# Reordering the first loads and spreading the norms, transposes and mixing of a decoder step on eight cores

## The chip, the cores and the metric

The program runs on all 8 NeuronCores of one Trainium2 chip, two dies of four cores. Every core runs the same instructions on its own batch element; the cores do not talk to each other. The time of one execution is the device time of the slowest core. Executions of one kernel mostly agree within 0.3%. There is a second, slower state, in which the cores of one die are granted a lower TensorE clock; runs in that state are set apart and only fast runs are compared with fast runs.

Engines in the profile: PE is TensorE (matmul), PEld its weight loads, DVE VectorE, ACT ScalarE, POOL GpSimd, SP the engine that issues most DMAs. L344 and so on are lines of the kernel; most operations go through helpers, so L344 is simply "a matmul", L347 "a transpose on TensorE", L362 a scalar_tensor_tensor on VectorE, L366 a copy by ScalarE.

## The reference, cut to what matters

One layer of a decoder. Per core: 2048 prompt rows and 128 sample rows of width 1024.

```python
h = rmsnorm(x, g_mix)
z = h @ w_in                       # u | v | p | q | gate_logits
u = gelu(u); vhat = layernorm(gelu(v), g_v, b_v)
a = (u * (tril(w_s[g]) @ vhat + b_s[g])) @ w_out_a       # per 128-row chunk, 4 groups
b = multiscale_pool(p, ...) @ w_out_b                    # trailing means, 2..16 rows
c = attend(q, memory K/V) @ w_out_c
x = x + (sig(g_a)*a + sig(g_b)*b + sig(g_c)*c) @ w_o
x = x + relu(rmsnorm(x) @ w_up)**2 @ w_down
y = rmsnorm(x, g_final)
```

The part that matters here is the first stage: rmsnorm of rows, then the projections v, q, p, u, and the spatial mixing. The bulk of the time (merge, `w_o`, MLP) is the same code in both kernels, but for the order in which the attention of the sample rows is slotted into the merge.

## The kernel before: the parts that the argument touches

Rows come in tiles of 128 (`x` tile t, 512 KB), four tiles to a block. For each tile: ScalarE squares and sums, VectorE and GpSimd make the reciprocal root (`norm_a`, `norm_b`), VectorE scales (`N`), TensorE transposes and an engine evicts the transpose, that is, copies it out of the matmul bank, into `hT` (`T`). Weights come in 30 chunks (2 MB in memory, cast to 1 MB by the DMA) into four slots; the first three are v, pq (p and q) and u. Chunks are issued from GpSimd's queue; rows and constants from SP's queue.

```python
def load_next(expect=None, after=()):
    # ... slot of the next chunk ...
    s.dma("pool", [(slots[sl][:, :], wpk[CH[nm]])], writes=[slot_b[sl]], owner=slot_b[sl], after=after)

def norm_load(t, src, after=()):
    xt, xb = ring("xst", xst, xst_b)                 # four row buffers
    s.dma("sp", [(xt, src)], writes=[xb], owner=xb, after=after)

def trans(t, dst, dst_bufs, col0, eng):              # T(t): eight transposes, one eviction
    for k in range(8):
        TR(b16[:, k*128:(k+1)*128], xn[:, k*128:(k+1)*128], [xnb], [bk_b])
    CP(eng, dst[:, :, col0:col0+128], ..., [bk_b], dst_bufs)

# start: constants, row 0, the norm gain broadcast to 128 partitions (512 KB), rows 1 to 3
s.dma("sp", [(bnd[:, B_ID:B_ID+128], cb[...])], ...)      # identity for the transposes
s.dma("sp", [(cstt[:], cst)], ...)                        # small constants
norm_load(0, xrow(0))
s.dma("sp", [(gb[:], gvec[0].partition_broadcast(128))], ...)
for t in BT[0][1:]:
    norm_load(t, xrow(t))
load_next("v", after=[cst_b])
# ...
for i in range(4):
    nb = norm_a([i]); norm_b(*nb)                    # statistics of row i
    if i >= 1:
        N(i - 1); T(i - 1)                           # scale and transpose row i-1
N(3)
load_next("pq", after=[slot_b[0]])                   # waits until v has landed
load_x(BT[1]); setup_loads(); mem_loads()
vmm(0); T(3)
for i in range(1, 4): vmm(i)                         # projection V
vfin()
load_next("u", after=[slot_b[1]])                    # waits until pq has landed
# ... Q(0), P(0..3), WIN(0), then the four U groups, with T(4..7) in between
```

`wpk`, `x` and so on are tensors in HBM. `after` makes the issuing queue wait for a landing. In these traces VectorE takes its instructions in program order, and that will matter: after the change row 0 has landed at 4.7 us, but VectorE scales it only at 31.5 us, just behind the statistics of row 1 (31.3 us), which stand before it in the program.

The softmax here doesn't subtract the row's maximum and nothing guards it: scores larger than these inputs give would overflow.

## Time and profile before

Median 977.1 us (975.6 to 977.5). The profiled execution, slowest core (core 7):

```profile
PE 915.6 (94%) x5312; PEld 472.1 (48%) x5312; DVE 383.7 (39%) x644; ACT 306.2 (31%) x535; POOL 267.7 (27%) x274
...
PE   0768889999999999999999999999999999999996
...
DMA  8891533804094122234050130402104040130134
```

The first line is the page's busy time of each engine in us, its share of the span and its instructions. The two others are 40 equal slices of the span (24 us each), one digit a slice, in tenths busy. TensorE is at 9 tenths or more nearly everywhere; it is open only in the first six slices, and at the very end, which the change does not touch. In the first two slices the DMA engines are nearly full.

The longest waits of TensorE up to 60.3 us (total us, number of waits, longest), and the chain of waits that ended last, from 0 to 62 us (start, us, what; longest pieces):

```profile
PE bank L347 <- DVE X L362: 25.3, 3, 18.3
PE bank L344 <- DMA slot<-wpk: 11.2, 2, 7.2
```

```profile
3.38 17.79 DMA X<-x
...
27.53 14.35 DMA slot<-wpk
...
42.42 17.68 DMA slot<-wpk
60.23 1.87 PE bank L344 x4
```

`X<-x` is the load of a row, `slot<-wpk` the load of a weight chunk, `bank` a bank of TensorE's output. Read the chain from the top: the third row (17.8 us to land), then chunk pq, then chunk u, one after the other, and only then the U groups can run. The timeline of TensorE shows the same two waits, and what a restart costs (columns: start, us, operation, count; in brackets the idle time before it and what ended it):

```profile
42.02 5.30 PE L344 MATMUL bank<-hT,slot 128*128 128x512 bf16 x16 [4.01 <-DMA slot<-wpk]
...
60.23 3.57 PE L344 MATMUL bank<-hT,slot 128*128 128x512 bf16 x8 [7.20 <-DMA slot<-wpk]
...
64.08 1.89 PE L344 MATMUL bank<-hT,slot 128*128 128x512 bf16 x8
```

The same eight matmuls take 3.6 us right after a 7.2 us wait and 1.9 us later. The Trainium skill ("TensorE: Matmul & The Clock Gate", Part 1) says that an idle TensorE falls back to half its clock and needs a few microseconds of work to get it back; this trace agrees, with a factor of 1.9 and a granted clock of 0.50 from 56.8 to 63.7 us.

### The profile page before, as it was taken

Reading aid. Unit: us, or ns where it says so; the run is one execution under the profiler, and the core shown is the slowest. Engines: PE = TensorE matmul, PEld = TensorE weight load, DVE = VectorE, ACT = ScalarE, POOL = GpSimd, SP = SyncE. Lnnn points to the kernel's source line nnn. Section 1 sums busy time; section 2 is a strip of 40 time slices with the busy share of each in tenths; the row PEclk is TensorE's granted clock in tenths of the full one; section 3 lists DMA queues with packets and bytes.
Section 4 is the critical chain, followed back from the end, with each engine's and each line's share of the span. In section 5 each row is a group of like instructions: output and inputs, shape, how many; then the busy total and the mean of one; then the engine's idle time right before and its main releaser. Section 6 shows DMA issues by size and latency. Waiting matters only on the chain.

```text
span 973.8 us, 15566 instructions; the slowest of 8 cores (967.0 to 973.8 us)
## 1 busy us (share of the span) xinstructions
PE 915.6 (94%) x5312; PEld 472.1 (48%) x5312; DVE 383.7 (39%) x644; ACT 306.2 (31%) x535; POOL 267.7 (27%) x274
## 2 busy tenths in 40 slices
PE   0768889999999999999999999999999999999996
PEld 0344555444555555545555544554445544455442
DVE  1366675423333322235532244222442234322476
ACT  2214454675322222225553200232003310033332
POOL 1103222614343343443332300222002310032243
PEclk9989999999999999999999999999999999999998
DMA  8891533804094122234050130402104040130134
GB/s 184 192 224 44 131 66 72 173 1 87 2 240 74 33 44 44 45 92 147 1 110 1 17 71 1 87 1 47 40 1 87 1 85 3 23 65 1 44 152 173
DMA packets 16536, 70.73 MB, mean 73 GB/s; under 512 B 1981, under 2 KB 3004, under 8 KB 12620
## 3 DMA queue, kind: packets, MB, share of 16 engines
q0 software_dynamic: 5472, 35.65, 20.6%
q1 hardware_dynamic: 10988, 34.09, 10.7%
q8 instruction: 44, 0.72, 0.3%
q14 instruction: 32, 0.26, 0.1%
HBM read 95.28 MB, written 10.22 MB: 108 GB/s over the span
## 4 chain that ended last, share of the span: by engine, by line
PE 88%; DMA 5%; DVE 2%; ACT 1%; issue 1%; POOL 1%; DVEq 0%; SPq 0%; POOLq 0%; ACTq 0%
PE bank L344 87%; DMA slot<-wpk 3%; DMA X<-x 2%; PE bank L347 1%; ACT X L350 1%; DVE X L362 1%; POOL stats L353 1%; ACT L350 0%; DVE X L359 0%; DVE CR L362 0%; DVE X L368 0%; DVE stats L547 0%; SPq L156 0%; DVEq L128 0%; DVE X L353 0%
## 5 line engine op out<-in xcount | busy, mean ns | idle before, releaser
L344 PE MATMUL bank<-hT,slot 128*128 128x436 bf16 (+3 forms) x2480 | 471.1, 349 | 12.9 <-DMA slot<-wpk 11.2
L344 PEld LDWEIGHTS bank<-hT,slot 128*128 128x128 bf16 x2480 | 240.3, 98 | 228.0 <-issue 20.9
L344 PE MATMUL bank<-slot,CR 128*128 128x512 bf16 (+1 forms) x1376 | 298.5, 378 | 0.1
L350 ACT ACTIVATE fA<-bank 128x436 f32<-128x436 f32 (+2 forms) x215 | 116.2, 544 | 361.6 <-PE bank L344 324.1
L344 PEld LDWEIGHTS bank<-slot,CR 128*128 128x128 bf16 x1376 | 134.0, 98 | 157.2 <-issue 0.2
L362 DVE SCALAR_TENSOR_TENSOR X<-bank,stats,X 128x512 f32<-128x512 f32 x136 | 102.0, 750 | 119.8 <-PE bank L344 119.8
L350 ACT ACTIVATE fW<-bank 128x436 f32<-128x436 f32 (+2 forms) x103 | 54.7, 533 | 166.4 <-PE bank L344 164.7
L353 POOL TENSOR_TENSOR CR<-fA 128x436 bf16<-128x436 f32 (+1 forms) x69 | 66.5, 964 | 109.1 <-ACT fA L350 104.8
L353 DVE TENSOR_TENSOR CR<-fA 128x436 bf16<-128x436 f32 (+1 forms) x51 | 31.2, 612 | 115.7 <-ACT fA L350 115.7
L353 DVE TENSOR_TENSOR fA<-bank,fA 128x436 f32<-128x436 f32 (+1 forms) x77 | 42.7, 603 | 79.8 <-PE bank L344 79.7
L353 POOL TENSOR_TENSOR stats<-stats,cstt 128x1 f32<-128x1 f32 (+3 forms) x30 | 35.4, 1181 | 119.4 <-DVE stats L359 77.9
L156 POOL DMA_DIRECT2D slot<-wpk x30 | 17.2, 573 | 182.8 <-PE bank L344 174.4
L350 ACT ACTIVATE CC<-X 128x1024 bf16<-128x1024 f32 x34 | 35.9, 1057 | 76.1 <-DVE stats L359 36.8
L344 PE MATMUL bank<-X,slot 128*128 128x436 bf16 (+1 forms) x240 | 57.1, 347 | 2.4 <-DVE X L353 2.0
L353 POOL TENSOR_TENSOR CR<-fW 128x436 bf16<-128x436 f32 (+1 forms) x37 | 35.1, 948 | 63.1 <-ACT fW L350 61.3
L344 PE MATMUL bank<-slot,hT 128*128 128x512 bf16 (+1 forms) x272 | 48.4, 334 | 2.1 <-DVE fA L362 1.2
L353 DVE TENSOR_TENSOR X<-bank,X 128x512 f32<-128x512 f32 (+2 forms) x39 | 26.7, 685 | 49.9 <-PE bank L344 25.5
L353 POOL TENSOR_TENSOR fA<-fA 128x436 f32<-128x436 f32 (+1 forms) x22 | 24.3, 1103 | 79.8 <-DVE fA L353 79.8
L353 DVE TENSOR_TENSOR CR<-fW 128x436 bf16<-128x436 f32 (+1 forms) x29 | 17.7, 612 | 66.7 <-ACT fW L350 66.7
L347 PE MATMUL bank<-bnd,X 128*128 128x128 bf16 x152 | 14.0, 242 | 29.6 <-DVE X L362 28.6
L353 DVE TENSOR_TENSOR fW<-bank,fW 128x436 f32<-128x436 f32 (+1 forms) x43 | 24.1, 603 | 42.8 <-PE bank L344 42.8
L344 PEld LDWEIGHTS bank<-slot,hT 128*128 128x128 bf16 x272 | 26.6, 100 | 21.6 <-issue 5.9
(90 smaller groups left out, 492.0 us busy)
## 6 DMA issues: line engine op xcount, KB each, us to landing
slot<-wpk POOLq DMA_DIRECT2D x30, 1024.0 KB, 12.2
X<-x SPq DMA_DIRECT2D x34, 512.0 KB, 8.5
y<-hT SPq DMA_DIRECT2D x17, 512.0 KB, 2.7
CR<-ck POOLq DMA_DIRECT2D x4, 512.0 KB, 8.4
CR<-cv POOLq DMA_DIRECT2D x4, 512.0 KB, 10.8
gb<-gvec SPq DMA_DIRECT2D x3, 512.0 KB, 9.1
CR<-mem SPq DMA_DIRECT2D x2, 512.0 KB, 24.2
fW<-wst SPq DMA_DIRECT2D x2, 256.0 KB, 12.3
```

The lines of the kernel that those rows point to most:

```text
L156: eng.dma_start(out=o_ap, in_=i_ap).then_inc(owner.sem, 16)
L344: s.op("pe", lambda e: e.matmul(out, lhsT=lhsT, rhs=rhs, start=start, stop=stop), R_, W_)
L347: s.op("pe", lambda e: e.transpose(out=out, in_=in_, identity=identb), R_ + [ident_b], W_)
L350: s.op("act", lambda e: e.activation(out=out, in_=in_, func=func, **kw), R_, W_)
L353: s.op(eng, lambda e: e.tensor_tensor(out=out, in0=in0, in1=in1, op=op), R_, W_)
L362: s.op("dve", lambda e: e.scalar_tensor_tensor(out=out, in0=in0, scalar=scalar, in1=in1, op0=op0, op1=op1), R_, W_)
```

## The change

Intent: keep TensorE fed in the first 270 us. (1) The first three weight chunks are queued at once, at the very start, on GpSimd's queue; row 0 goes out before them, rows 1 to 3 behind them on SP's queue. (2) The 512 KB broadcast of the norm gain becomes a 4 KB row, which TensorE spreads over the partitions with two f32 matmuls against a row of ones; the 512 KB of broadcast bias rows is treated alike, with one-row f32 matmuls that add the bias into the spatial-gate constants. (3) Norms, transposes (many now evicted by ScalarE) and mixing are spread between the projections. (4) Set-up loads move behind what is needed first. The core of the diff:

```diff
+        onef = CC[1][0:1, 0, :]                      # a row of ones
+        norm_load(0, xrow(0))
+        grow = oT[0:1, 0, 0:2048].bitcast(F32)
+        s.dma("sp", [(grow, gvec[0].unsqueeze(0))], writes=grow_b, owner=grow_b[0])
+        load_next("v")
+        load_next("pq")
+        load_next("u")
+        s.dma("sp", [(cstt[:], cst)], writes=[cst_b], owner=cst_b)
         s.dma("sp", [(bnd[:, B_ID:B_ID + 128], ...)], ...)
-        s.dma("sp", [(cstt[:], cst)], writes=[cst_b], owner=cst_b)
-        norm_load(0, xrow(0))
-        s.dma("sp", [(gb[:], gvec[0].partition_broadcast(128))], ...)
         for t in BT[0][1:]:
             norm_load(t, xrow(t))
-        load_next("v", after=[cst_b])
+        for n in range(2):                           # gain row -> 128 partitions
+            MM(bk[:, :], onef, grow[:, n*512:(n+1)*512], True, True, ...)
+            CP("act", gb[:, n*512:(n+1)*512], bk[:, :], [bk_b], [gb_b])
 ...
+        def setup_mm(i):
+            for g in range(4):
+                MM(o, bvb[:, g*128:(g+1)*128], wsf[i][:, g, :], True, False, ...)
+                MM(o, onef, bsrow[:, i*512 + g*128:...], False, True, ...)
 ...
-        load_next("pq", after=[slot_b[0]])
-        load_x(BT[1])
+        load_x(BT[1][0:2], after=[slot_b[1]])
         setup_loads()
-        mem_loads()
+        load_x(BT[1][2:4], after=[slot_b[2]])
 ...
-        load_next("u", after=[slot_b[1]])
 ...                                                  # the block loop, written out:
+        us.append(U(1, 2))
+        T(nx[0], "act")
+        MIX(1, 1, *us[1])
+        ...
```

The loop over the first four rows (`norm_a`, `norm_b`, `N(i-1)`, `T(i-1)`) is unchanged.

More of the change, by code (lines that the diff above doesn't have):

```diff
@@ L457, in build_program @@
         BT = [[0, 1, 2, 3], [4, 5, 6, 7], [8, 9, 10, 11], [12, 13, 14, 15]]
+        onef = CC[1][0:1, 0, :]
+        MEMSET("dve", onef, 1.0, [CC_b[1]])
+        norm_load(0, xrow(0))
+        grow = oT[0:1, 0, 0:2048].bitcast(F32)
+        grow_b = oT_b[0][0:4]
+        s.dma("sp", [(grow, gvec[0].unsqueeze(0))], writes=grow_b, owner=grow_b[0])
[3 more added lines that the diff above has]
+        s.dma("sp", [(cstt[:], cst)], writes=[cst_b], owner=cst_b)
         s.dma("sp", [(bnd[:, B_ID:B_ID + 128], cb[:, B_ID:B_ID + 128])], writes=[ident_b], owner=ident_b)
-        s.dma("sp", [(cstt[:], cst)], writes=[cst_b], owner=cst_b)
-        norm_load(0, xrow(0))
-        s.dma("sp", [(gb[:], gvec[0].partition_broadcast(128))], writes=[gb_b], owner=gb_b)
         for t in BT[0][1:]:
             norm_load(t, xrow(t))
-        x_b = [norm_src[t][1] for t in BT[0]]
-        load_next("v", after=[cst_b])
         MEMSET("pool", ones, 1.0, [ones_b])
         MEMSET("pool", qbd, 0.0, [qbd_b])
+        for n in range(2):
+            bk, bk_b = pb()
+            MM(bk[:, :], onef, grow[:, n * 512:(n + 1) * 512], True, True, grow_b + [CC_b[1]], [bk_b])
+            CP("act", gb[:, n * 512:(n + 1) * 512], bk[:, :], [bk_b], [gb_b])
         wst_t, wst_tb = tW()
@@ L472, in build_program, with wst_load @@
         wsf_b = [wst_tb, wst_t2b]
-        cfg = kvs[1].bitcast(F32)
-        cfg_b = kvs_b[1]
-        cfg_o = s.buf("cfgdma")
+        bvb, bvb_b = kvs[1][:, 1024:2048].bitcast(F32), s.buf("bvb")
+        wpf, wpf_b = kvs[1][:, 3072:3584].bitcast(F32), s.buf("wpf")
+        bsrow = xlo16[0:1, 6144:8192].bitcast(F32)
+        bsrow_b = [vhs_b, sth_b, prs_b]
         mem_o = s.buf("memdma")
         sth_o = s.buf("sthdma")
-        bvb, wpf = cfg[:, 0:512], cfg[:, 1536:1792]
-        bsb = [cfg[:, 512:1024], cfg[:, 1024:1536]]
+        def wst_load(i):
+            s.dma("sp", [(wsf[i], wst[:, i * 512:(i + 1) * 512].rearrange("p (g i) -> p g i", g=4))], writes=[wsf_b[i]], owner=wsf_b[i])
@@ L481, in setup_loads @@
         def setup_loads():
-            for i in range(2):
-                s.dma("sp", [(wsf[i], wst[:, i * 512:(i + 1) * 512].rearrange("p (g i) -> p g i", g=4))], writes=[wsf_b[i]], owner=wsf_b[i])
-            s.dma("sp", [(bsb[i], bsx[i * 512:(i + 1) * 512].partition_broadcast(128)) for i in range(2)] +
-                  [(bvb, gbv[512:1024].partition_broadcast(128)), (wpf, wpb)], writes=cfg_b, owner=cfg_o)
-        def setup_ops():
-            for i in range(2):
-                TT("dve", wsf[i], wsf[i], maskT.unsqueeze(1).broadcast_to([128, 4, 128]), ALU.mult, [wsf_b[i], cst_b], [wsf_b[i]])
-                CP("pool", wsT[i], wsf[i], [wsf_b[i]], [wsT_b[i]])
-            for ft in range(2):
-                TS("dve", wpbd[:, ft, :], wpf[:, ft * 128:(ft + 1) * 128], pscol[:, ft:ft + 1], None, ALU.mult, None, cfg_b + [cst_b], [wpbd_b])
@@ L494, in setup_mm @@
-        def setup_mm():
-            for i in range(2):
-                bk, bk_b = pb()
-                for g in range(4):
-                    MM(bk[:, g * 128:(g + 1) * 128], bvb[:, g * 128:(g + 1) * 128], wsf[i][:, g, :], True, True, cfg_b + [wsf_b[i]], [bk_b])
-                TT("dve", CC[i][:].rearrange("p g i -> p (g i)"), bk[:, :], bsb[i], ALU.add, [bk_b] + cfg_b, [CC_b[i]])
+            wst_load(0)
+            s.dma("sp", [(bvb, gbv[512:1024].partition_broadcast(128))], writes=[bvb_b], owner=bvb_b)
@@ new lines, in setup_loads, with setup_ops @@
+            s.dma("sp", [(bsrow, bsx.unsqueeze(0))], writes=bsrow_b, owner=vhs_b)
+        def setup_ops(i):
+            TT("dve", wsf[i], wsf[i], maskT.unsqueeze(1).broadcast_to([128, 4, 128]), ALU.mult, [wsf_b[i], cst_b], [wsf_b[i]])
+            CP("pool", wsT[i], wsf[i], [wsf_b[i]], [wsT_b[i]])
+        def setup_mm(i):
+            bk, bk_b = pb()
+            for g in range(4):
+                o = bk[:, g * 128:(g + 1) * 128]
+                MM(o, bvb[:, g * 128:(g + 1) * 128], wsf[i][:, g, :], True, False, [bvb_b, wsf_b[i]], [bk_b])
+                MM(o, onef, bsrow[:, i * 512 + g * 128:i * 512 + (g + 1) * 128], False, True, bsrow_b + [CC_b[1]], [bk_b])
+            CP("act", CC[i][:].rearrange("p g i -> p (g i)"), bk[:, :], [bk_b], [CC_b[i]])
@@ L501, in tX, with setup_wp @@
+        def setup_wp():
+            for ft in range(2):
+                TS("dve", wpbd[:, ft, :], wpf[:, ft * 128:(ft + 1) * 128], pscol[:, ft:ft + 1], None, ALU.mult, None, [wpf_b, cst_b], [wpbd_b])
         def tX():
@@ L645, in WIN, with U @@
                 CP("dve", pm[:, ft, c0:c1], bk[:, 0:c1 - c0], [bk_b], [pm_b[ft][j]])
-        def U(j, g):
+        def U(j, g, late=False):
             w, wb = W("u", 8)
@@ L653, in U, with ge @@
                 MM(bk[:, 0:n], w[:, k, g * 128:(g + 1) * 128], hT[:, k, c0:c1], k == 0, k == 7, htb(j) + [wb], [bk_b])
-            ug, ug_b = tA()
-            ACT(ug[:, 0:n], bk[:, 0:n], AF.Gelu_apprx_tanh, [bk_b], [ug_b])
-            return ug, ug_b
+            def ge():
+                ug, ug_b = tA()
+                ACT(ug[:, 0:n], bk[:, 0:n], AF.Gelu_apprx_tanh, [bk_b], [ug_b])
+                return ug, ug_b
+            return ge if late else ge()
         def MIX(j, g, ug, ug_b):
@@ L728, in kvs_load @@
             i = g % 2
-            s.dma("pool", [(kvs[i][:, 0:2048], ck[g])], writes=[kvs_b[i][0]], owner=kvs_b[i][0])
-            s.dma("pool", [(kvs[i][:, 2048:4096], cv[g])], writes=[kvs_b[i][1]], owner=kvs_b[i][1])
+            s.dma("pool", [(kvs[i][:, 0:2048], ck[g])], writes=[kvs_b[i][0]] + ([bvb_b] if i else []), owner=kvs_b[i][0])
+            s.dma("pool", [(kvs[i][:, 2048:4096], cv[g])], writes=[kvs_b[i][1]] + ([wpf_b] if i else []), owner=kvs_b[i][1])
         samp = {}
@@ L814, in WPO, with T @@
             CP("dve", wq[:].rearrange("p f c -> p (f c)"), bk[:, 0:256], [bk_b], [wq_b])
-        def T(t):
-            trans(t, hT, [hT_b[t]], t * 128, "dve")
+        def T(t, eng="dve"):
+            trans(t, hT, [hT_b[t]], t * 128, eng)
         def load_x(ts, after=()):
@@ L844, in build_program @@
         vfin()
-        load_next("u", after=[slot_b[1]])
-        na = norm_a(BT[1])
-        norm_b(*na)
         Q(0)
@@ L851, in build_program @@
             vout(i)
-        N(4)
-        N(5)
-        WIN(0)
-        setup_ops()
-        load_next("kv", after=[slot_b[2]])
-        us = []
-        for g in range(4):
-            us.append(U(0, g))
-            T(4 + g)
-            if g < 2:
-                N(6 + g)
-        setup_mm()
+        na = norm_a([4, 5])
+        WIN(0)
+        norm_b(*na)
+        us = [U(0, 0)]
+        setup_ops(0)
+        nb = norm_a([6, 7])
+        us.append(U(0, 1))
+        N(4)
+        norm_b(*nb)
@@ L864, in build_program @@
+        us.append(U(0, 2))
+        N(5)
+        T(4, "act")
+        us.append(U(0, 3))
+        N(6)
+        setup_mm(0)
+        MIX(0, 0, *us[0])
+        T(5, "act")
+        MIX(0, 1, *us[1])
+        N(7)
+        T(6, "act")
+        MIX(0, 2, *us[2])
+        MIX(0, 3, *us[3])
         load_x(BT[2])
-        for g in range(4):
-            MIX(0, g, *us[g])
+        load_next("kv")
+        mem_loads()
+        wst_load(1)
+        s.dma("sp", [(wpf, wpb)], writes=[wpf_b], owner=wpf_b)
@@ L867, in build_program @@
         hst = hist_loads()
-        for j in range(1, 4):
-            nx = BT[j + 1] if j < 3 else []
-            vt = BT[j] + ([16] if j == 3 else [])
-            if j == 3:
-                n16 = norm_a([16])
-                norm_b(*n16)
-            if j == 3:
-                S(1, 0)
-            if j == 2:
-                na = norm_new(4)
-                norm_sq(na, nx[0])
-                norm_sq(na, nx[1])
-            P(BT[j][0])
-            P(BT[j][1])
-            Q(j)
-            if j == 2:
-                S(0, 0)
-            if j == 3:
-                S(1, 1)
-            if j == 3:
-                N(16)
-                s.dma("sp", [(gb[:], gbv.partition_broadcast(128))], writes=[gb_b], owner=gb_b)
-            if j == 2:
-                S(0, 1)
-            P(BT[j][2])
-            P(BT[j][3])
-            if j == 3:
-                T(16)
-            if j >= 2:
-                AV(j - 2, 0)
-            if j == 2:
-                norm_sq(na, nx[2])
-                norm_sq(na, nx[3])
-                norm_b(*na)
-                N(nx[0])
-            if j == 3:
-                Q(4)
-                P(16)
-            if j >= 2:
-                AV(j - 2, 1)
-            vmm, vfin, vout = V(vt)
-            if j == 1:
-                na = norm_new(4)
-            for i in range(len(vt)):
-                vmm(i)
-                if j == 1:
-                    norm_sq(na, nx[i])
-                if j == 2 and i < 3:
-                    N(nx[1 + i])
-                if j == 2 and i >= 2:
-                    T(nx[i - 2])
-            vfin()
-            if j == 1:
-                norm_b(*na)
-                mst = norm_a([100, 101])
-                norm_b(*mst)
-                N(nx[0])
-            if j == 2:
-                load_x([16])
-            if j == 3:
-                load_next("mrg1")
-                load_next("mrg2")
-            for i in range(len(vt)):
-                vout(i)
-            WIN(j)
-            if j == 3:
-                WIN(4)
-                u4 = U4()
-            us = []
-            for g in range(4):
-                us.append(U(j, g))
-                if j == 1:
-                    if g < 3:
-                        N(nx[g + 1])
-                    if g >= 1:
-                        T(nx[g - 1])
-                    if g == 1:
-                        norm_c(100, gm, gm_b)
-                    if g == 2:
-                        norm_c(101, gm, gm_b)
-                if j == 2 and g < 2:
-                    T(nx[2 + g])
-            if j == 1:
-                load_x(BT[3])
-                for t in range(2):
-                    trans(100 + t, hmT, hmT_b, t * 128, "dve")
-            if j == 2:
-                hist_ops(*hst)
-                kvs_load(0)
-                kvs_load(1)
-            if j == 3:
-                load_next("mrg3")
-                WPO(0)
-            for g in range(4):
-                MIX(j, g, *us[g])
-                if j == 1 and g == 1:
-                    T(nx[3])
-            if j == 1:
-                KV()
-                load_next("mrg0")
-            if j == 3:
-                MIX4(*u4)
-            flush()
@@ new lines, in build_program @@
+        nx = BT[2]
+        P(4)
+        P(5)
+        T(7, "act")
+        P(6)
+        Q(1)
+        P(7)
+        na = norm_new(4)
+        vmm, vfin, vout = V(BT[1])
+        for i in range(4):
+            vmm(i)
+            norm_sq(na, nx[i])
+        vfin()
+        norm_b(*na)
+        for i in range(4):
+            vout(i)
+        WIN(1)
+        us = [U(1, 0)]
+        N(nx[0])
+        us.append(U(1, 1))
+        MIX(1, 0, *us[0])
+        N(nx[1])
+        us.append(U(1, 2))
+        T(nx[0], "act")
@@ new lines, in build_program @@
+        MIX(1, 1, *us[1])
+        mst = norm_a([100, 101])
+        norm_b(*mst)
+        N(nx[2])
+        us.append(U(1, 3))
+        T(nx[1], "act")
+        MIX(1, 2, *us[2])
+        N(nx[3])
+        load_x(BT[3])
+        MIX(1, 3, *us[3])
+        nx = BT[3]
+        P(8)
+        T(10, "act")
+        P(9)
+        T(11, "act")
+        norm_c(100, gm, gm_b)
+        P(10)
+        Q(2)
+        norm_c(101, gm, gm_b)
+        P(11)
+        trans(100, hmT, hmT_b, 0, "act")
+        na = norm_a(nx[0:2])
@@ new lines, in build_program @@
+        vmm, vfin, vout = V(BT[2])
+        vmm(0)
+        trans(101, hmT, hmT_b, 128, "act")
+        norm_b(*na)
+        setup_ops(1)
+        vmm(1)
+        nb = norm_a(nx[2:4])
+        N(nx[0])
+        norm_b(*nb)
+        vmm(2)
+        setup_mm(1)
+        KV()
+        load_next("mrg0")
+        vmm(3)
+        N(nx[1])
+        vfin()
+        S(0, 0)
+        S(0, 1)
+        for i in range(4):
+            vout(i)
+        WIN(2)
+        AV(0, 0)
+        T(nx[0])
+        us = [U(2, 0, True)]
@@ new lines, in build_program @@
+        AV(0, 1)
+        us[0] = us[0]()
+        setup_wp()
+        us.append(U(2, 1))
+        N(nx[2])
+        MIX(2, 0, *us[0])
+        us.append(U(2, 2))
+        T(nx[1], "act")
+        MIX(2, 1, *us[1])
+        N(nx[3])
+        us.append(U(2, 3))
+        T(nx[2], "act")
+        MIX(2, 2, *us[2])
+        load_x([16])
+        MIX(2, 3, *us[3])
+        kvs_load(0)
+        kvs_load(1)
+        P(12)
+        P(13)
+        T(15)
+        S(1, 0)
+        Q(3)
+        S(1, 1)
+        n16 = norm_a([16])
@@ new lines, in build_program @@
+        norm_b(*n16)
+        P(14)
+        P(15)
+        AV(1, 0)
+        AV(1, 1)
+        N(16)
+        s.dma("sp", [(gb[:], gbv.partition_broadcast(128))], writes=[gb_b], owner=gb_b)
+        hist_ops(*hst)
+        vt = BT[3] + [16]
+        vmm, vfin, vout = V(vt)
+        vmm(0)
+        vmm(1)
+        T(16)
+        vmm(2)
+        Q(4)
+        vmm(3)
+        P(16)
+        vmm(4)
+        vfin()
+        load_next("mrg1")
+        load_next("mrg2")
+        for i in range(5):
+            vout(i)
@@ L972, in build_program @@
+        WIN(3)
+        WIN(4)
+        u4 = U4()
+        us = [U(3, 0), U(3, 1)]
+        MIX(3, 0, *us[0])
+        us.append(U(3, 2))
+        MIX(3, 1, *us[1])
+        us.append(U(3, 3))
+        load_next("mrg3")
+        WPO(0)
+        MIX(3, 2, *us[2])
+        MIX4(*u4)
+        MIX(3, 3, *us[3])
+        flush()
         s.dma("sp", [(gb[:], gvec[2].partition_broadcast(128))], writes=[gb_b], owner=gb_b)
@@ L1033, in build_program @@
             (1, 0): lambda: AV(2, 0, tX),
-            (1, 1): lambda: (AV(2, 1, tX), S(3, 0)),
-            (2, 0): lambda: (S(3, 1), SA1(0), SA1(1)),
-            (2, 1): lambda: (AV(3, 0, tX), SA2(0), SA2(1)),
-            (0, 2): lambda: (AV(3, 1, tX), SA2b(0), SA2b(1), kvs_load(2), kvs_load(3)),
-            (1, 2): lambda: (SA3(0), SA3(1)),
+            (1, 1): lambda: AV(2, 1, tX),
+            (2, 0): lambda: (S(3, 0), SA1(0)),
+            (2, 1): lambda: (S(3, 1), SA1(1)),
+            (0, 2): lambda: (AV(3, 0, tX), SA2(0), SA2(1)),
+            (1, 2): lambda: (AV(3, 1, tX), SA2b(0), SA2b(1), kvs_load(2), kvs_load(3)),
+            (2, 2): lambda: (SA3(0), SA3(1)),
             (0, 3): lambda: (SA1(2), SA1(3)),
```

## The prediction

> **What bounds the kernel.** TensorE. The page shows it busy 916 of 974 us; by windows it never stops from 267 to 940 us. The change touches what comes before, so only idle time there can be won. TensorE's gaps before 267 us sum to 49 us: 18.3 us until the first transpose, 18.7 us from there to 60.2 us, 12.1 us afterwards.
>
> Of the second sum, 11.2 us is waiting for two weight chunks (waits: slot<-wpk, 4.0 and 7.2 us). The chunks come one after the other: chunk v was issued at 5.5 us and landed at 21.9, pq 27.5 to 41.9, u 42.4 to 60.1, because each waits for the one before and shares the DMA engines with setup data (memory rows, broadcast bias rows, gains: about 3 MB not needed yet). Restarting costs too: eight 512-column matmuls took 3.6 us at 60.2 us, against 1.9 us warm.
>
> **What the change does.**
> 1. v, pq and u are issued together at about 1 us. Later in this trace queued chunks land 4.4 to 6 us apart. The 512 KB broadcast of the norm gain (9.1 us to land) becomes a 4 KB row and two f32 matmuls, in idle time. Setup loads shrink and move behind.
> 2. Three chunks (24 packets per DMA engine, 0.7 to 0.8 us each) plus four rows (32 packets, 0.16 to 0.4 us) and constants still need about 28 us of saturated DMA. The Trainium skill ("DMA: Bandwidth & Descriptors", Queues, rings and completion order) says that each engine takes turns between queues packet by packet; the packet records agree: between 13 and 20 us about 15 chunk packets and 14 row packets end per us. A chunk packet takes three to four times as long as a row packet, so rows are slowed: I expect x3 at 25 to 30 us (before: 23.1), u at 26 to 31 us (before: 60.1).
> 3. So the first stage becomes bound by rows, not weights: after x3 come Square, pow, scaling, transpose (5 to 8 us in this trace), then V, Q, P and windows, about 16 us of TensorE. The first U group should start at 46 to 54 us, central 50, instead of 60.2, and warm. Gain about 12 us.
> 4. Spreading norms and transposes, half of them evicted by ScalarE, should cut the 12.1 us of later gaps (2.0 us before a transpose at 97.7 us, 2.0 us in the merge at 207.7 us) to about 4, and some cold clock with them (clock 0.94 at 80 to 100 us): gain 9 to 10 us.
> 5. Added: eight one-row f32 matmuls for the bias; the f32 ones of before took 2.0 us together, so minus 2 us.
>
> Sum: 977 - 12 - 9.5 + 2, about 957 us. Range 946 to 968. Chances: faster by over 2% 0.52, within 2% 0.46, slower 0.02.
>
> **What would show it.** Step 1: u lands near 28 us, TensorE waits under 2 us for slot<-wpk. Step 2: x1 to x3 land later than before. Step 3: the chain at the start names X<-x, not slot<-wpk; U starts near 50 us. Step 4: later gaps under 5 us. Step 5: TensorE busy within 3 us of before. From the merge on, the same durations.
>
> **What would make it wrong.** If rows slip past 32 us, U starts after 55 us and the gain halves. If the row queue gets ahead of the weights, U starts near 42 us and the time nears 948. If ScalarE evictions delay the GELUs, the later gaps stay.

## The result, and the profile after

974.1 us median (973.8 to 974.7), against 976.4 us (975.2 to 977.5) of the kernel before on the same chip. Ratios here and below are the mean time of one kernel's fast runs over that of the other's of the same rounds, so not quite the ratio of the medians quoted: 0.9978, 95% interval 0.9961 to 0.9995. The change is worth 0.2%, where I had forecast 2%.

```profile
PE 918.2 (94%) x5332; PEld 473.9 (49%) x5332; DVE 378.0 (39%) x633; ACT 322.1 (33%) x553; POOL 275.3 (28%) x276
...
PE   1499999999999999999999999999999999999996
...
DMA  8527236903294122234050130402204040130134
```

From the third slice on it is full now, but the first two fell from "07" to "14". The waits up to 60.3 us and the chain up to 62 us, on the same core as before:

```profile
PE bank L347 <- DVE X L362: 29.2, 3, 24.8
PE bank L344 <- DMA X<-gvec: 4.4, 1, 4.4
```

```profile
2.81 27.14 DMA X<-x
30.04 1.16 ACT X L350 x2
31.48 1.30 DVE X L362
34.89 1.20 DVE X L362
36.22 1.03 PE bank L347 x8
38.09 1.20 DVE X L362
40.44 3.41 PE bank L344 x8
44.71 10.61 PE bank L344 x56
...
```

No wait for a chunk is left. In its place stands one row of 27 us: x1, a DMA of 512 KB, is issued at 2.8 us and lands at 30.0. The timeline of TensorE:

```profile
33.02 1.01 PE L347 MATMUL bank<-bnd,X 128*128 128x128 bf16 x8 [24.84 <-DVE X L362]
36.22 1.01 PE L347 MATMUL bank<-bnd,X 128*128 128x128 bf16 x8 [2.19 <-DVE X L362]
39.43 1.01 PE L347 MATMUL bank<-bnd,X 128*128 128x128 bf16 x8 [2.19 <-DVE X L362]
...
59.20 5.35 PE L344 MATMUL bank<-hT,slot 128*128 128x512 bf16 x24
```

The first transpose runs at 33.0 us (before: 18.3), the first U group at 59.2 us (before: 60.2). The landings, from the DMA issues of the two traces (us from the span's start, slowest core):

| | issued, landed before | issued, landed after |
|---|---|---|
| x0 | 2.0, 8.3 | 1.1, 4.7 |
| constants (70 KB) | 1.5, 4.9 | 2.0, 14.3 |
| x1 | 2.9, 15.2 | 2.8, 30.0 |
| x2 | 3.4, 21.2 | 3.3, 31.3 |
| x3 | 4.1, 23.1 | 4.2, 32.5 |
| chunk v | 5.5, 21.9 | 1.6, 14.5 |
| chunk pq | 27.5, 41.9 | 2.3, 21.6 |
| chunk u | 42.4, 60.1 | 2.8, 30.2 |

One trap of reading the slowest core alone: I worked the prediction out on core 7, whose chunk u landed at 60.1 us. Over the eight cores of that execution u landed at 50.8 to 60.1 us. So here are medians over the eight cores of the profiled execution of each kernel: when x3 and u had landed, when row 3 was transposed (T3), when the first U group started, how long it took from there to the first matmul of the merge, and from the merge to `w_o`. From `w_o` to the end every kernel takes 545.6 us (median, undisturbed dies).

| us, median of 8 cores | x3 landed | u landed | T3 | first U | U to merge | merge to w_o |
|---|---|---|---|---|---|---|
| before | 21.5 | 54.5 | 29.3 | 54.7 | 118.1 | 250.7 |
| after | 31.1 | 29.4 | 40.1 | 55.6 | 117.6 | 249.6 |

On the median core the first U group even starts 0.9 us later than before; the later stages give 1.6 us. All of the expected 12 us at the start are gone. (T3 has one more condition: V's first eight matmuls stand before it on TensorE, so it waits for chunk v too. That matters in the runs below that issue the chunks late.)

### The profile page after: what moved, and what is told of

Read it like the earlier page. It is cut to its first block, busy times and chain, and to the rows that moved or that the text cites. A ratio compares the mean times of both kernels' runs of the same rounds, so it can differ in the third digit from the quotient of the medians.

```text
span 972.3 us, 15604 instructions; the slowest of 8 cores (967.7 to 972.3 us)
## 1 busy us (share of the span) xinstructions
PE 918.2 (94%) x5332; PEld 473.9 (49%) x5332; DVE 378.0 (39%) x633; ACT 322.1 (33%) x553; POOL 275.3 (28%) x276
## 4 chain that ended last, share of the span: by engine, by line
PE 89%; DMA 4%; DVE 2%; ACT 2%; issue 1%; POOL 0%; DVEq 0%; SPq 0%; POOLq 0%; ACTq 0%
PE bank L344 87%; DMA X<-x 3%; PE bank L347 2%; DMA CR<-ck 1%; DVE X L362 1%; ACT X L350 1%; ACT L350 1%; ACT fA L350 0%; DVE stats L559 0%; DVE X L359 0%; POOL stats L353 0%; ACT hT L366 0%; DVEq L128 0%; ACT CR L350 0%; SPq L156 0%
## 5 line engine op out<-in xcount | busy, mean ns | idle before, releaser
L353 POOL TENSOR_TENSOR stats<-stats,cstt 128x1 f32<-128x1 f32 (+3 forms) x32 | 39.7, 1240 | 137.4 <-DVE stats L359 95.3
L353 DVE TENSOR_TENSOR CR<-fA 128x436 bf16<-128x436 f32 (+1 forms) x51 | 31.2, 612 | 115.1 <-ACT fA L350 115.1
```

Of the source, the lines that this page charges most:

```text
L353: s.op(eng, lambda e: e.tensor_tensor(out=out, in0=in0, in1=in1, op=op), R_, W_)
```

## The experiments

Theory A: the three chunks, queued ahead, hold up the rows; TensorE needs all four rows before it can go on, so the wait moved from the chunks to the rows. Rival B: the sum of bytes bounds; no order can feed the first stage sooner. Theory C: part of the loss is program order, since row 0 landed at 4.7 us and was transposed at 33.0. Rival D: the queue is a gain, and the spread stages give it back.

### e1: the same three chunks, queued behind the rows

```diff
-        load_next("v"); load_next("pq"); load_next("u")      # ahead of the rows
 ...
         for i in range(4):
             nb = norm_a([i]); norm_b(*nb)
+            if i == 2:
+                load_next("v"); load_next("pq"); load_next("u")
```

> The changed kernel, with the three chunks issued together after the row statistics of x2 (so behind the four rows) instead of ahead of them. Theory A (the gain was lost because the queued chunks hold up rows x1 to x3, and the transposes, V, Q and P start only behind the last row): x3 lands by 14 us instead of 32.5, u at 28 to 34 us (30.2), the transpose of row 3 starts by 26 us instead of 43.7, the first U group at 38 to 43 us instead of 59.2, time 953 to 960 us. Rival B (it is the sum of DMA bytes: no order can feed the first stage before about 30 us, and the work behind takes as long as before): first U at 54 us or later, time 970 us or more.

962.7 us median, ratio to the kernel before 0.9866 (0.9844 to 0.9889): 11 us less than the change, by moving three lines. x3 landed at 12.5 us (median core), the first U group started at 45.0 us. Rival B falls: it had 54 us or later, and 970 us or more. Of theory A's numbers only x3 was met; u (40.8 us), T3 (29.5), U and the time all came later than I had written, and the waits show why:

```profile
PE bank L347 <- DVE X L362: 9.9, 4, 4.9
PE bank L344 <- DMA slot<-wpk: 6.6, 1, 6.6
```

The chunks went out only at 17.1 us on the slowest core, because in GpSimd's queue they stood behind the statistics of x2, and v became the wait.

### e5 and e7: no chunk ahead, one chunk ahead

e5 issues the chunks as soon as x1 has landed (after the statistics of row 0 in GpSimd's queue, with `after=` row 1). e7 is e5 with v alone left at the start.

```diff
         for i in range(4):
             nb = norm_a([i]); norm_b(*nb)
+            if i == 0:
+                for c in ("v", "pq", "u"):                  # e7: only "pq", "u" here, "v" at the start
+                    load_next(c, after=[norm_src[1][1]])
```

> The changed kernel, with the three chunks issued together once row x1 has landed, without waiting for any statistics (in e1 the issue stood behind the statistics of x2 in GpSimd's queue, went out only at 17.1 us, and TensorE then waited 6.6 us for v). Theory A (the order on the DMA engines decides): chunks issued near 10.5 us, x3 landed by 15 us, v by 21, u by 34; wait for v under 1 us; first U group at 38 to 42 us (45.9 in e1, 59.2 in the change); time 955 to 959 us. If it is the sum of bytes that bounds, the time stays at 962 us.

> As e5, but chunk v is issued at the start, ahead of the rows, and only pq and u behind x1: the dose between no chunk ahead (e5) and three (the change). Theory A: each chunk ahead keeps the last row back by about 6 us (8 packets per DMA engine of 0.7 to 0.8 us): x3 at 17 to 22 us (12.8 with none ahead in e1, 32.5 with three), first U at 40 to 46 us, time 956 to 963 us. If what holds the rows is not the chunks (cold start, small constants), x3 stays above 28 us or equals that of e5.

The chip had die 1 at a lower clock (0.98) in nearly every run, so only die 0 is read. The median core of die 0 spanned 953.9 us in e5 (11 runs) and 958.4 us in e7 (7 runs in which die 0 had its full clock), against 971.4 us for the kernel before (11 runs); each figure is the median over the runs. e5 was run again on another chip:

> e5 again, unchanged: in the first look every run of its chip had one die at a lower clock. Undisturbed cores then spanned 951 to 955 us, against 967 to 972 us for the change. Expected 956 to 959 us in the fast state.

957.7 us median, ratio 0.9809 (0.979 to 0.9827), as expected; whether the gain reaches 2% is open. The chunks were issued at 11.6 us, TensorE waited 1.9 us for v on the slowest core, and u landed at 36.0, all a little later than I had written. Its chain of waits up to 45 us:

```profile
2.82 6.98 DMA X<-x
...
12.24 10.96 DMA slot<-wpk
23.34 3.57 PE bank L344 x8
...
27.73 10.39 PE bank L344 x56
```

x1 takes 7.0 us where it took 27.1. The dose is clear in the landing of x3 (medians of 8 cores): 12.2 us with no chunk ahead (e5 again), 18.5 with one (e7), 31.1 with three (the change). That is 6.3 us for the first chunk and (31.1 - 18.5) / 2 = 6.3 us for each of the other two. Theory A holds, with its size. (e7's figure includes its slow die, whose rows landed as on the other: 17.9 to 18.9 us against 18.0 to 19.3.)

### b1 and b2: the queue alone, on the kernel before

b1 puts the three chunks ahead of everything in the kernel before; b2 puts them behind the statistics of x2, as e1 does. Nothing else of the change is in either.

```diff
-        load_next("v", after=[cst_b])
-        load_next("pq", after=[slot_b[0]])
-        load_next("u", after=[slot_b[1]])
+        load_next("v"); load_next("pq"); load_next("u")      # b1: first of all; b2: at i == 2 of the row loop
```

> The kernel before, with one part of the change alone: v, pq and u issued together ahead of the rows. Theory A: the wait only moves, from the chunks to the rows: u lands near 31 us, x3 at 31 to 36 us, no wait for slot<-wpk, first U at 58 to 63 us (60.2), time 973 to 980 us (before 976.4). Rival D (the queue by itself is worth 10 us or more and the spreading of the later stages gives it back): 962 to 967 us.

> The kernel before, with v, pq and u issued together behind the four rows, and nothing else of the change. Theory A: x3 at 15 to 18 us (the broadcast gain is still loaded), u at 30 to 36 us, first U at 40 to 45 us instead of 60.2, time 956 to 962 us, so most of what the whole change was meant to win comes from this one move. Rivals B and D: 968 us or more.

b1: 980.9 us, ratio 1.0044 (1.0029 to 1.0059). The queue by itself makes the kernel slower, by 4 us, a little beyond what I had written: x3 landed at 34.2 us and the first U group started at 62.4 us (medians). The one wait that counts:

```profile
PE bank L347 <- DVE X L362: 40.7, 3, 36.3
```

b2: 971.0 us, ratio 0.9941 (0.9928 to 0.9955). The direction is theory A's, the size is not: I expected 956 to 962. Its chunks were issued at 19 us (again behind GpSimd's statistics), and v landed only at 31.2, as the next rows and, from 25 us on, the set-up loads of the kernel before (about 3 MB) shared the DMA engines. TensorE waited for v:

```profile
PE bank L344 <- DMA slot<-wpk: 8.8, 1, 8.8
```

U started at 52.1. u had landed by then (47.2), and TensorE waited for no other chunk.

Rival D falls with b1: the rest of the change does not give a gain back, it makes good a loss. (The two ran on different chips; by the ratios to the kernel before, too, they are 0.7% apart.) From b1 to the change the time falls by 980.9 - 974.1 = 6.8 us, and the first U group starts 62.4 - 55.6 = 6.8 us sooner.

### e3 and e10: the order of the first rows' instructions

VectorE's queue holds the scaling of row 0 behind the statistics of row 1, so row 0 waits for x1. e3 puts `N(i)`, `T(i)` behind their own statistics. e10 queues all four statistics first, then the four scalings, with the transposes evicted by ScalarE.

```diff
             nb = norm_a([i]); norm_b(*nb)
-            if i >= 1:
-                N(i - 1); T(i - 1)
-        N(3)
+            N(i)                                    # e3
+            if i < 3: T(i)
```

> The changed kernel, with the scaling and transpose of row i placed before the statistics of row i+1 instead of behind them; loads untouched. Theory C (part of the loss is program order: row 0, landed at 4.7 us, is transposed only at 33.0 us because VectorE's queue holds its scaling behind the statistics of row 1, and then four rows go one after the other, 3.2 us each): row 0 transposed at 22 to 25 us (identity lands at 21.4), row 3 at 40 to 41.5 us instead of 43.7, time 970 to 972.5 us, that is 2 to 4 us less. If the order does not matter: row 3 at 43 to 44 us and 973 to 975 us.

> The changed kernel with its loads untouched; the first block's statistics of all four rows are queued before the first scaling, and ScalarE evicts those transposes, so VectorE's four scalings (1.3 us each) follow each other without waiting for a transpose in between. Theory C (after the last row the change spends 11.1 us until the transpose of row 3, because scaling, transpose and eviction of the four rows run one after the other at 3.2 us a row): x3 stays at 31 to 33 us, transpose of row 3 at 38.5 to 40.5 us instead of 43.7, first U at 54 to 56 us instead of 59.2, time 969 to 971 us. If the rows' landing alone counts: no change, 973 to 975 us.

e3: 971.9 us, ratio 0.9953 (0.9938 to 0.9967), about 2 us less than the change, within what was expected. Row 0 was transposed at 16.6 us on the median core and at 21.0 on core 7, for which I had written 22 to 25; row 3 at 37.6 instead of 40.1 (median). Theory C accounts for 2 us.

e10 is a miss: 973.5 us, ratio 0.9965 (0.9948 to 0.9981), not to be told from the change. On core 7, the change's slowest, row 3 came sooner (40.0 instead of 43.7 us), but on the median core it did not (39.9 against 40.1), and the stretch from U to the merge grew by 1.4 us (119.0 against 117.6). The 11 us from the landing of x3 to T3 that I had read on core 7 are 9 us on the median core, and packing the scalings hardly shortened them (8.6 us). No run was made on why the later stretch grew; the traces show one part of it, a stretch of half clock behind the f32 products on all eight cores of e10 and on three of the change's (next section).

### e4: one bias matmul instead of four

The profile after has a cost that I had sized at 2 us. Before, eight f32 products; after, sixteen, half of them with one row:

```profile
70.60 2.00 PE L344 MATMUL bank<-fW,CR 128*128 128x128 f32 x16
```

```profile
66.56 0.38 PE L344 MATMUL bank<-fW,CR 128*128 128x128 f32 x2
66.88 0.48 PE L344 MATMUL bank<-X,CC 1*128 1x128 f32 x2
67.29 0.49 PE L344 MATMUL bank<-fW,CR 128*128 128x128 f32 x2
67.71 0.48 PE L344 MATMUL bank<-X,CC 1*128 1x128 f32 x2
```

An f32 product is two instructions in the trace. Before, 8 products in a row took 2.0 us, 0.25 us each; after, where products and one-row products alternate, they start 0.41 us apart, so 16 take 6.6 us. e4 adds the bias with one 512-column matmul in front of the four products:

```diff
+            MM(bk[:, :], onef, bsrow[:, i*512:(i+1)*512], True, False, ...)
             for g in range(4):
-                MM(o, bvb[...], wsf[i][:, g, :], True, False, ...)
-                MM(o, onef, bsrow[...128 columns...], False, True, ...)
+                MM(o, bvb[...], wsf[i][:, g, :], False, g == 3, ...)
```

> The changed kernel, with the bias row of each spatial-gate set added by one 512-column one-row f32 matmul ahead of the four f32 products instead of by four 128-column ones in between. The f32 matmuls of the two sets take 6.6 us in the change against 2.0 us in the kernel before (prediction: 4.0), 0.41 us each when weights alternate. Theory F (that excess lies on the critical path and is the stationary operand's reload): the two sets take 3.5 to 4.5 us, time 971 to 972.5 us instead of 974.1. If it is hidden or not reload: 973.5 us or more.

```profile
64.92 1.12 PE L344 MATMUL bank<-X,CC 1*128 1x512 f32 x2
65.97 1.16 PE L344 MATMUL bank<-fW,CR 128*128 128x128 f32 x8
```

(Core 3, on the undisturbed die.) A set takes 2.05 us (64.92 to 66.97) instead of 3.3, both sets about 4.1 instead of 6.6. The stretch from U to the merge falls from 117.6 to 115.2 us, so the saving is on the critical path. The whole time can't be compared: this chip had its slow die, and the change itself did not run on it (die 0: 966.8 us for the median core, 971.4 us for the kernel before; the ratio of 0.9962, 0.9933 to 0.9991, is over three runs whose die 1 was at 0.98 as well). That alternating operands are what costs, rather than the eight products fewer, is argued from the spacing and not separated.

The traces show a second cost of the alternating products, which I had overlooked. On core 3 of the change, 16 matmuls right behind the second set, and the next 16 of the same shape:

```profile
117.53 3.49 PE L344 MATMUL bank<-slot,CR 128*128 128x256 bf16 x16
120.86 1.91 PE L344 MATMUL bank<-CR,slot 128*128 128x256 bf16 x16
```

On cores 3 to 5 the granted clock is 0.50 for 3.4 us from the end of that set, although TensorE had been busy for all but 0.15 us of the 3.4 us before. U to the merge takes 119.3 us on these three cores and 117.4 to 117.6 on the other five. In e10 this happens on all eight cores, behind one of the two sets; in e4 (die 0) and e8, whose sets are shorter, on none. So the one bias matmul may save more than its own 2.5 us; no run was made to test that.

### e9: evictions back on VectorE

```diff
-        T(4, "act")          # and 11 more, the two memory tiles included
+        T(4)
```

> The changed kernel, with all transposes that it evicts by ScalarE evicted by VectorE again (as before the change), nothing else. Theory G (the later gaps, 10.8 us against the 4 predicted, stay because ScalarE's evictions stand behind GELUs): gaps behind the first U fall to 8 us or less, time 971 to 972.5 us. Rival H (each gap is a chain of small waits that only moves, scaling on VectorE being the common one): gaps 9 to 13 us, time 973 to 976 us.

975.8 us, ratio 0.9991 (0.9975 to 1.0007). The gaps from U to the merge grow to 9.4 us from 8.5 (medians), and the stretch to 120.1 us from 117.6. ScalarE's evictions are not what keeps the gaps; they shorten this stretch by 2.4 us at the median, and by 1.0 us if the cores without a half-clock stretch are compared (118.5 against 117.5). (The whole times, taken on different chips, do not separate the two kernels: the intervals of their ratios overlap.) Theory G falls. That leaves H, the chain of small waits, not refuted but not proven either.

### e6 and e8: candidates

e6 is e5 with e4's bias and ScalarE evictions in the unchanged row loop. e8 issues the chunks once x0 has landed, takes the row loop of e10 and the bias of e4.

```diff
         for t in BT[0][1:]:
             norm_load(t, xrow(t))
+        for c in ("v", "pq", "u"):                          # e8
+            load_next(c, after=[norm_src[0][1]])
 ...
         for i in range(4):
             nb = norm_a([i]); norm_b(*nb)
-            if i >= 1:
-                N(i - 1); T(i - 1)
-        N(3)
+        for i in range(4):
+            N(i)
+            if i < 3: T(i, "act")
```

> A candidate to beat both kernels: e5 with the one-matmul bias of e4, and with the transposes of the first four rows evicted by ScalarE, so that VectorE's scalings do not wait for the transposes of the row before (3.2 us per row in the change). Expected: rows one after the other in 2.3 us, first U at 36 to 40 us, f32 sets 2.5 us shorter, time 950 to 956 us; if the eviction does not matter it is e5 less e4's gain.

> Candidate: chunks issued together as soon as row x0 has landed (near 6 us, with x1 to x3 already queued), statistics first and ScalarE evictions as in e10, one bias matmul per set as in e4. Expected: x3 at 13 to 17 us, u at 29 to 33 us, transpose of row 3 at 20 to 23 us, first U at 36 to 39 us (42.1 in e5), f32 sets 2 us each, time 947 to 953 us on a chip in the fast state.

e6 ran with the slow die: 953.7 us on die 0's median core, no better than e5 (953.9). The eviction by ScalarE in that loop made row 3 later (27.4 us against 24.9) and ate the bias's gain: rows went 4.9 us apart, where I had written 2.3, and U started at 43.0.

e8: 954.8 us median (954.5 to 955.8), ratio 0.9778 (0.976 to 0.9797), faster than the kernel before by 2.2% and than the change by some 19 us. It is 2 us above my range, and T3 and U are just above theirs. Medians: x3 at 15.6 us, T3 at 24.0, first U at 39.2, U to merge 115.6. Its chain up to 45 us:

```profile
3.68 14.44 DMA X<-x
18.20 1.16 ACT X L350 x2
22.04 1.29 DVE X L362
24.47 2.86 PE bank L344 x8
```

It still starts with a row: on that slowest core x3 landed at 18.1 us, since the chunks' packets came between. On the two cores where x3 landed soonest (12.1 and 12.8) the first U group started at 38.8 and 37.7, on the slowest at 42.3.

| time, us | chunks | x3 landed | T3 | first U | median | ratio to before |
|---|---|---|---|---|---|---|
| before | one after the other | 21.5 | 29.3 | 54.7 | 976.4 | |
| b1 | ahead, nothing else changed | 34.2 | 45.0 | 62.4 | 980.9 | 1.0044 |
| the change | ahead | 31.1 | 40.1 | 55.6 | 974.1 | 0.9978 |
| e3 | ahead, rows not lagged | 31.0 | 37.6 | 53.2 | 971.9 | 0.9953 |
| b2 | behind, nothing else changed | 15.2 | 34.7 | 52.1 | 971.0 | 0.9941 |
| e1 | behind statistics of x2 | 12.5 | 29.5 | 45.0 | 962.7 | 0.9866 |
| e5 again | behind x1 | 12.2 | 24.8 | 40.0 | 957.7 | 0.9809 |
| e8 | behind x0, and the rest | 15.6 | 24.0 | 39.2 | 954.8 | 0.9778 |

Among the kernels that carry the whole change, the time follows the start of the first U group nearly one to one: from the change to e5 again U moves by 15.6 us and the time by 16.4.

## Why the prediction was wrong

The prediction was 957 us (946 to 968), the result 974.1, outside the range.

- Step 1, the chunks: right. u landed at 30.2 us (said: 26 to 31), and TensorE waited for no chunk at all up to 60 us.
- Step 2, the rows are slowed by taking turns with the chunks: the mechanism was right, the size too small. I had x3 at 25 to 30 us; it landed at 32.5 (30.6 to 32.5 over the cores). I had costed the sum of packets, about 28 us of full DMA engines, and placed x3 inside it; as the last in the row queue it comes at the end of it, 1.3 to 2.7 us behind u on every core. The skill's page ("DMA: Bandwidth & Descriptors", Queues, rings and completion order) speaks of turns by packet, and the packet records after the change agree: from 6 to 20 us, 247 chunk packets (8 KB written each) and 249 packets of the row queue ended. But most of those 249 were the constants' packets of 560 and 256 bytes. A small packet takes a turn like a large one, so 70 KB of constants took 12.4 us to land on core 7, and x1 moved only as the constants got through (200 of the 249 were constants). This is not what made x3 late, though: on core 6 those 70 KB had landed at 5.5 us, ahead of the chunks, and x1 at 22.5, yet x3 came at 30.6. No run moved the constants alone.
- Step 3 is the step that failed first and cost most. "After x3 ... 5 to 8 us, then ... about 16 us of TensorE. The first U group should start at 46 to 54 us, central 50." The 16 us were right (T3 to U: 15.5 us). The term of 5 to 8 us was mis-sized: from x3 to T3 it was 11.2 us on the profiled core and 9.0 on the median core, and already 8.4 on the profiled core before the change. Rows 1 to 3 land within 2.5 us of each other, and then all four rows go through scaling, transpose and eviction one after the other (transposes at 33.0, 36.2, 39.4 and 43.7 us), where I had counted the last row alone; e3 shows that 2.5 us of this is the order of the instructions, the rest is not taken apart. And x3 itself came 5 us later than the middle of my range. So U started at 59.2 us. Besides, "instead of 60.2" was the slowest core's; on the median core U had started at 54.7 us before. The gain of 12 us (10.2 for the start, 1.7 for a warm TensorE) became 1.0 us of start on core 7 and a loss of 0.9 us on the median core; the warm start came, and is counted in the next stretch. e1, e5 and e7 show the cause: the same kernel with all chunks, or two of the three, behind the rows starts U 10 to 16 us sooner.
- Step 4, later gaps: failed too. The gaps were to bring 8 of its 9 to 10 us: they were to fall from 12.1 to about 4 us; on core 7 they were 11.0 us after, 8.5 of them from U to the merge. I had taken for granted that spreading removes waits; it exchanged 13 of 0.2 to 2.0 us for 16 of 0.2 to 1.5 us (those over 0.15 us). What each of them hangs on I did not settle; e9 shows only that it is not ScalarE's evictions. The other half of this step, the cold clock, was right: the busy time by windows, before and then after, shows the granted clock (third number from the right) rise to 1.00. Before, it was 0.50 for 3.4 us from 97.8 us, right behind the wait of 2.0 us. (This is core 7; three of the eight cores have the other half-clock stretch shown under e4.)

```profile
80.00:100.00 20.00, 17.01 (x145) 8.82 (x143) 12.98 (x24) 10.88 (x21) 2.75 (x3) 0.94 0.17 53
```

```profile
80.00:100.00 20.00, 19.06 (x173) 10.48 (x171) 11.92 (x24) 12.45 (x23) 5.64 (x5) 1.00 0.77 199
```

- Step 5, added work: the sign was right, the term too small. The f32 products grew by 4.6 us (2.0 to 6.6), not by 2. TensorE's busy time rose by 2.6 us in all, within the 3 us said.

The sum on core 7: start -1.0 us, U to merge +0.2 (an estimate: two stretches of 3.4 us at half the clock are gone, worth 1.7 us each, and the f32 products take 4.6 us more; with 0.2 us less of gaps that makes +1.0, and 0.8 us stays open), merge to `w_o` -0.7, together -1.5 us, which is the difference of the two profiled spans (973.8 and 972.3 us). My own list of what would make it wrong had the case, "if rows slip past 32 us", and still allowed half the gain there; measured were 1.0 us on core 7 and none on the median core.

## What to carry to other kernels

When a chain needs several loads before it can start, issue them in the order in which the chain uses them: queueing the large loads first took away every wait for them and put the same wait on the small ones behind, here 6.3 us for each 2 MB chunk ahead. Queues that share the DMA engines were not served by importance but took turns packet by packet here (247 packets against 249), so what these runs could move was when something is issued; and an issue placed in a busy engine's instruction queue waits for that engine's earlier work too (17.1 us in e1, although x1 had landed at 10.3 us). Work out the start on several cores, not on the slowest alone: before the change the landing of chunk u differed by 9 us between cores, and the first U group started 5.5 us sooner on the median core than on the slowest, nearly half of the gain that I had counted.

## What the Trainium skill lacked or had wrong

- "DMA: Bandwidth & Descriptors" (Queues, rings and completion order) gives turn-taking at packet granularity but not what it does to unequal packets. Here 8 KB chunk packets (mean 0.8 us each) and the row queue's packets, 200 of them constants of 256 and 560 bytes, had equal counts, 247 and 249 between 6 and 20 us on core 7: 70 KB of constants took 12.4 us to land beside the chunks there (3.6 to 13.1 us over the cores), 3.4 us without them.
- The same page has no number for what a queued casting load costs the loads behind it. Here each 2 MB chunk ahead delayed the last row by 6.3 us.
- No page that I found has a time for f32 matmuls in sequence, beyond the number of passes: 128-column products took 0.25 us each one after another, and started 0.41 us apart when they alternated with one-row products.
- "TensorE: Matmul & The Clock Gate" (Part 1) agreed on the factor: 3.6 us cold against 1.9 us warm for the same eight matmuls. It puts the fall to half clock after an idle window of about 3.4 us. Here the granted clock fell to 0.50 behind single waits of 2.0 to 2.5 us (seven of eight cores before the change, 97.8 us on core 7), and on three of eight cores after it at the end of 3.3 us of alternating f32 and one-row products, with no wait at all.
